# A store behind the last load: one load instead of two, and a wait on VectorE instead of on the load's first part

## Chip, cores, metric

One core of one Trainium2 chip. The metric is the device time of one execution in microseconds (us); the median over several executions is quoted. The profile's span runs from the core's first to its last recorded instruction.

## The reference

The first half of each head's 64 elements is rotated by tables of cosines and sines; the second half is passed on.

```python
# x: (16, 512, 16, 64) float32; cos, sin: (512, 32) float32
x1, x2 = x[..., :32], x[..., 32:]
first  = x1[..., :16] * cos[..., :16] - x1[..., 16:] * sin[..., :16]
second = x1[..., :16] * sin[..., :16] + x1[..., 16:] * cos[..., :16]
out = concatenate([first, second, x2], axis=-1)
```

33.5 MB are read and 33.5 MB are written.

## The kernel before

The data are four tiles of 128 partitions x 16 rows (64 KB a partition, 8 MB a tile). A ring in SBUF has three slots, so tile 3 goes into tile 0's slot once tile 0 is stored. VectorE rotates a tile in place, in two pieces of 8 rows, with four instructions each. All loads and stores are issued by one queue (SP).

```python
    K = 16; NS = 3; KC = K // 2; KL = 14
    # ...
    load(0)
    load(1)
    load(2, 0, KC)
    # ... tables for cosine and sine ...
    def rotate(t, lo, hi):
        # ...
        nc.vector.tensor_mul(out=b_t, in0=x1, in1=s)            # L96
        nc.vector.tensor_mul(out=x1, in0=x1, in1=c)             # L97
        nc.vector.tensor_sub(out=x1[..., 0:Q], ...)             # L98
        nc.vector.tensor_add(out=x1[..., Q:HF], ...)            # L101

    def turn(t):
        rotate(t, 0, KC)
        rotate(t, KC, K)
        return store(t)

    turn(0)
    load(2, KC, K)
    near = load(3, 0, KL)
    load(3, KL, K)
    tc.add_manual_dep(turn(1).ins, near.ins.name, ...,   # the store of tile 1 waits for `near`
        reason="the store follows the loads at the DMA engines")
    turn(2)
    turn(3)
```

The queue's order is load 0, 1, half of 2, store 0, the other half of 2, load 3 (14 rows, then 2), store 1, 2, 3. Nothing in the data makes store 1 wait for load 3; only the declared dependence does.

Of the kernel before, what the change touches and what calls it, by code (L numbers as in the profile page):

```python
# [1 line left out]

# [4 lines left out]


@with_exitstack
def kernel(  # L10
    ctx: ExitStack,
    tc: tile.TileContext,
    x: bass.AP,
    cos: bass.AP,
    sin: bass.AP,
    out: bass.AP,
):
    nc = tc.nc
    fp32 = mybir.dt.float32
    P = 128  # L20
    B, S, H, D = x.shape
    Q = D // 4
    HF = D // 2



    K = 16
    T = B * S // (P * K)
    PB = S // K
    REP = P // PB  # L30
    R = H * D
    NS = 3
    KC = K // 2
    KL = 14

    xf = x.rearrange("b s h d -> (b s h d)").rearrange("(t p f) -> t p f", t=T, p=P)
    of = out.rearrange("b s h d -> (b s h d)").rearrange("(t p f) -> t p f", t=T, p=P)
    cosf = cos.rearrange("(p k) j -> p (k j)", k=K)
    sinf = sin.rearrange("(p k) j -> p (k j)", k=K)

    const_pool = ctx.enter_context(tc.tile_pool(name="const", bufs=1))
    b_pool = ctx.enter_context(tc.tile_pool(name="bp", bufs=1, space=bass.MemoryType.PSUM))


    ring = const_pool.tile([P, NS, K, H, D], fp32)
    stage = const_pool.tile([P, 2, K, HF], fp32)
    spun = const_pool.tile([P, 2 * K, Q], fp32)
    packed = const_pool.tile([PB, 2 * K, Q], fp32)
    table = const_pool.tile([P, 2, K, 2, Q], fp32)

    def rows(t, lo, hi):
        return ring[:, t % NS, lo:hi].rearrange("p k h d -> p (k h d)")

    def load(t, lo=0, hi=K):
        return nc.sync.dma_start(out=rows(t, lo, hi), in_=xf[t, :, lo * R : hi * R])

    def store(t, lo=0, hi=K):
        return nc.sync.dma_start(out=of[t, :, lo * R : hi * R], in_=rows(t, lo, hi))


    nc.vector.memset(stage[:, :, :, 0:Q], 0.0)  # L61
    spread = stage.rearrange("(j b) t k i -> j b t (k i)", b=REP)
    nc.gpsimd.dma_start(out=spread[:, 0, 0], in_=cosf)  # L63
    nc.gpsimd.dma_start(out=spread[:, 0, 1], in_=sinf)  # L64
# [7 lines that stand above are left out]
    PQ = PB // REP  # L72
    nc.vector.stream_shuffle(  # L73
        out=spun[:],
        in_=stage.rearrange("p t k j -> p (t k) j")[:, :, 0:Q],
        mask=[j % PQ * REP for j in range(PB)],
    )
    for q in reversed(range(REP)):
        n = PQ * (q + 1)
        nc.vector.tensor_copy(out=packed[0:n], in_=spun[q * PB : q * PB + n])  # L80

    for r in range(REP):
        nc.vector.tensor_copy(  # L83
            out=table[r * PB : (r + 1) * PB].rearrange("p t k c j -> p (t k) c j"),
            in_=packed.unsqueeze(2).to_broadcast((PB, 2 * K, 2, Q)),
        )
    C = table[:, 0].rearrange("p k c j -> p k (c j)")
    Sn = table[:, 1].rearrange("p k c j -> p k (c j)")

    def rotate(t, lo, hi):  # L90
        x1 = ring[:, t % NS, lo:hi, :, 0:HF]
        c = C[:, lo:hi].unsqueeze(2).to_broadcast((P, hi - lo, H, HF))
        s = Sn[:, lo:hi].unsqueeze(2).to_broadcast((P, hi - lo, H, HF))
        b_full = b_pool.tile([P, KC, H, HF], fp32, name="b_t")
        b_t = b_full[:, 0 : hi - lo]
        nc.vector.tensor_mul(out=b_t, in0=x1, in1=s)  # L96
        nc.vector.tensor_mul(out=x1, in0=x1, in1=c)  # L97
        nc.vector.tensor_sub(  # L98
            out=x1[:, :, :, 0:Q], in0=x1[:, :, :, 0:Q], in1=b_t[:, :, :, Q:HF]
        )  # L100
        nc.vector.tensor_add(  # L101
            out=x1[:, :, :, Q:HF], in0=x1[:, :, :, Q:HF], in1=b_t[:, :, :, 0:Q]
        )

    def turn(t):
        rotate(t, 0, KC)
        rotate(t, KC, K)
        return store(t)

    turn(0)  # L110
    load(2, KC, K)
    near = load(3, 0, KL)
    load(3, KL, K)

    tc.add_manual_dep(
        turn(1).ins,
        near.ins.name,
        mybir.DependencyInfo(mybir.DependencyClass.Sync, mybir.DependencyReason.DATA),
        reason="the store follows the loads at the DMA engines",
    )  # L120
    turn(2)
    turn(3)


# [1 line left out]
_INS = ['x', 'cos', 'sin']  # L126
_OUTS = [((16, 512, 16, 64), 'float32')]


# [23 lines left out]
```

## Time and profile before

| | before |
|---|---|
| time, median (6 runs) | 161.45 us (161.37 to 161.53) |
| span of the profile | 160.3 us, on a run of 162.1 us |
| DMA queue, share of 16 engines | 97.6% |
| VectorE busy | 112.4 us, 70% |

The lines are in the prediction below. VectorE matters only through when it lets the queue issue something. The profile fell on an execution 0.6 us slower than the median.

### The profile page before, as it was taken

The numbers are of one execution on the slowest core, as the hardware profiler recorded it, in microseconds if no ns is written. First come the engines' busy times: TensorE is split into PE (matmuls) and PEld (weight loads), VectorE is DVE, ScalarE is ACT, GpSimd is POOL, SyncE is SP. The second block draws the span as 40 slices with busy tenths as digits, with TensorE's granted clock in tenths as the row PEclk, the third lists the DMA queues.
The fourth block names the chain that finished last, engine by engine and source line by source line (L and its number), as shares of the span: only waits on it lengthen the run. The fifth ranks groups of instructions, "written<-read, shape, count | busy, mean of one in ns | idle before, by whom it ended". The sixth has DMA issues, their size and how long they took to land.

```text
span 160.3 us, 113 instructions
## 1 busy us (share of the span) xinstructions
DVE 112.4 (70%) x43; POOL 1.4 (1%) x6
## 2 busy tenths in 40 slices
DVE  1000959999999999999999999999999950000000
POOL 3000000000000000000000000000000000000000
DMA  7969969699699996999999995996996996996990
GB/s 262 540 262 540 491 294 523 278 507 491 294 392 441 474 523 262 523 392 392 499 482 458 458 444 253 546 523 262 523 523 262 523 507 278 523 507 278 523 507 16
DMA packets 1504, 67.24 MB, mean 419 GB/s; under 512 B 192, under 2 KB 192, under 8 KB 224
## 3 DMA queue, kind: packets, MB, share of 16 engines
q1 hardware_dynamic: 1440, 67.11, 97.6%
q0 software_dynamic: 64, 0.13, 0.2%
HBM read 33.69 MB, written 33.55 MB: 419 GB/s over the span
## 4 chain that ended last, share of the span: by engine, by line
DVE 59%; DMA 14%; issue 7%; DVEq 1%
DVE b_t L96 22%; DVE ring L97 22%; DMA ring<-in_x_dram 14%; DVE ring L101 10%; DVE ring L98 4%; DVEq L148 1%; DVEq L96 0%
## 5 line engine op out<-in xcount | busy, mean ns | idle before, releaser
L96 DVE TENSOR_TENSOR b_t<-ring,table 128x4096 f32<-128x4096 f32 x8 | 35.5, 4432 | 2.1 <-DMA ring<-in_x_dram 1.9
L97 DVE TENSOR_TENSOR ring<-ring,table 128x4096 f32<-128x4096 f32 x8 | 35.4, 4424 | 0.3
L98 DVE TENSOR_TENSOR ring<-ring,b_t 128x2048 f32<-128x2048 f32 x8 | 18.3, 2287 | 0.3
L101 DVE TENSOR_TENSOR ring<-ring,b_t 128x2048 f32<-128x2048 f32 x8 | 18.2, 2280 | 0.0
L73 DVE LOAD_MASK_SELECT spun<-stage x1 | 0.0, 14 | 14.4 <-DMA stage<-in_sin_dram 14.4
L83 DVE COPY table<-packed 32x1024 f32<-32x1024 f32 x4 | 2.7, 684 | 0.1
L80 DVE COPY packed<-spun 32x512 f32<-32x512 f32 (+3 forms) x4 | 1.7, 416 | 0.1
L61 DVE MEMSET stage<- 128x512 f32 x1 | 0.5, 485 | 0.9 <-PEq L137 0.9
L73 DVE STREAM_SHUFFLE spun<-stage 128x512 f32<-128x512 f32 x1 | 0.7, 723 | 0.0
L63 POOL DMA_DIRECT2D stage<-in_cos_dram x1 | 0.6, 649 | 1.3 <-DVE stage L61 1.3
L64 POOL DMA_DIRECT2D stage<-in_sin_dram x1 | 0.5, 532 | 0.0
L137 POOL MEMSET const-float32-0.0<- 128x1 f32 x1 | 0.1, 93 | 0.2 <-issue 0.2
L137 POOL MEMSET const-bfloat16-1.0<- 128x1 bf16 x1 | 0.1, 95 | 0.0
L137 POOL MEMSET const-uint8-127<- 128x1 uint8 x1 | 0.1, 93 | 0.0
L137 POOL MEMSET const-float32-1.0<- 128x1 f32 x1 | 0.1, 92 | 0.0
## 6 DMA issues: line engine op xcount, KB each, us to landing
ring<-in_x_dram SPq DMA_DIRECT2D x2, 4096.0 KB, 41.4
ring<-in_x_dram SPq DMA_DIRECT2D x1, 7168.0 KB, 26.4
ring<-in_x_dram SPq DMA_DIRECT2D x1, 1024.0 KB, 28.5
stage<-in_cos_dram POOLq DMA_DIRECT2D x1, 64.0 KB, 9.0
stage<-in_sin_dram POOLq DMA_DIRECT2D x1, 64.0 KB, 13.4
out_dram<-ring SPq DMA_DIRECT2D x4, 25.6
ring<-in_x_dram SPq DMA_DIRECT2D x2, 32.0
```

What stands on the lines that cost most here:

```text
L61: nc.vector.memset(stage[:, :, :, 0:Q], 0.0)
L63: nc.gpsimd.dma_start(out=spread[:, 0, 0], in_=cosf)
L64: nc.gpsimd.dma_start(out=spread[:, 0, 1], in_=sinf)
L73: nc.vector.stream_shuffle(out=spun[:], in_=stage.rearrange("p t k j -> p (t k) j")[:, :, 0:Q], mask=[j % PQ * REP for j in range(PB)],)
L80: nc.vector.tensor_copy(out=packed[0:n], in_=spun[q * PB : q * PB + n])
L83: nc.vector.tensor_copy(out=table[r * PB : (r + 1) * PB].rearrange("p t k c j -> p (t k) c j"), in_=packed.unsqueeze(2).to_broadcast((PB, ...
L96: nc.vector.tensor_mul(out=b_t, in0=x1, in1=s)
L97: nc.vector.tensor_mul(out=x1, in0=x1, in1=c)
L98: nc.vector.tensor_sub(out=x1[:, :, :, 0:Q], in0=x1[:, :, :, 0:Q], in1=b_t[:, :, :, Q:HF])
L101: nc.vector.tensor_add(out=x1[:, :, :, Q:HF], in0=x1[:, :, :, Q:HF], in1=b_t[:, :, :, 0:Q])
L137: nc = _bacc.Bacc("TRN2", target_bir_lowering=False, num_devices=1)
L148: with _tile.TileContext(nc) as tc:
```

## The change

The last load goes out whole, which saves a DMA of small packets. The store behind it, which must not come late, is released by a point in VectorE's work on tile 2 that falls shortly before the load's end. To have such a point, the second half of tile 2 is rotated in two pieces, rows 8 to 12 and 13 to 15.

```diff
-    KL = 14
+    KM = 13
...
-    turn(0)
+    rotate(0, 0, KC)
+    rotate(0, KC, K)
+    store(0)
     load(2, KC, K)
-    near = load(3, 0, KL)
-    load(3, KL, K)
+    load(3)
+    rotate(1, 0, KC)
+    rotate(1, KC, K)
+    behind_loads = store(1)
+    rotate(2, 0, KC)
+    near = rotate(2, KC, KM)      # rotate now returns its last instruction
+    rotate(2, KM, K)
+    store(2)
     tc.add_manual_dep(
-        turn(1).ins,
+        behind_loads.ins,
         near.ins.name, ...
```

More of the change, by code (lines that the diff above doesn't have):

```diff
@@ L100, in rotate @@
         )
-        nc.vector.tensor_add(
+        return nc.vector.tensor_add(
             out=x1[:, :, :, Q:HF], in0=x1[:, :, :, Q:HF], in1=b_t[:, :, :, 0:Q]
         )
-    def turn(t):
-        rotate(t, 0, KC)
-        rotate(t, KC, K)
-        return store(t)
-    turn(0)
-    load(2, KC, K)
-    near = load(3, 0, KL)
-    load(3, KL, K)
+    rotate(0, 0, KC)
+    rotate(0, KC, K)
+    store(0)
+    load(2, KC, K)
+    load(3)
[6 more added lines that the diff above has]
+    store(2)
     tc.add_manual_dep(
-        turn(1).ins,
+        behind_loads.ins,
         near.ins.name,
@@ L120 @@
     )
-    turn(2)
-    turn(3)
+    rotate(3, 0, KC)
+    rotate(3, KC, K)
+    store(3)
 _INS = ['x', 'cos', 'sin']
```

## The prediction

> **What bounds the kernel now.** I read the page's header, its rows by slice and its queue table first, to see which resource is full.
>
> ```profile
> span 160.3 us, 113 instructions
> ...
> DVE 112.4 (70%) x43; POOL 1.4 (1%) x6
> ...
> DVE  1000959999999999999999999999999950000000
> ...
> GB/s 262 540 262 540 491 294 523 278 507 491 294 392 441 474 523 262 523 392 392 499 482 458 458 444 253 546 523 262 523 523 262 523 507 278 523 507 278 523 507 16
> DMA packets 1504, 67.24 MB, mean 419 GB/s; under 512 B 192, under 2 KB 192, under 8 KB 224
> ...
> q1 hardware_dynamic: 1440, 67.11, 97.6%
> ```
>
> One DMA queue fills 97.6% of sixteen engines over the whole span, while VectorE is busy for 70% and stops a fifth before the end. The jumping GB/s row is only an artefact: whole packets are counted in the slice in which they begin. Averaged over nearly the whole stream the engines are full:
>
> ```profile
> core 0: us, DVE busy (x) POOL busy (x), PEclk, DMA share, GB/s
> 2.30:158.40 156.10, 111.87 (x42) 0.58 (x2) 1.00 0.99 425
> ...
> 158.40:160.30 1.90, 0.00 (x0) 0.00 (x0) 1.00 0.00 0
> ```
>
> In the single packet records of the trace I looked for holes. There are none after the start: a 65,536-byte packet takes 2.418 us and the next on its engine starts 2.414 us after it, whether load or store, from the first packet at 1.74 us to the last store data at 158.4 to 158.9 us. So the span is 1.7 us of start, about 157 us of uninterrupted stream, and about 1.5 us of last landing and closing. The chain of waits on the page names VectorE for 59%, but it is a poor guide here: it ends in VectorE's last instruction and does not follow the last store. The queue's own waits and the order of issues tell more.
>
> ```profile
> SPq L58 <- DMA ring<-in_x_dram: 46.5, 2, 25.6
> SPq L148 <- DMA out_dram<-ring: 28.3, 1, 28.3
> ...
> ring<-in_x_dram SPq DMA_DIRECT2D x1, 7168.0 KB, 26.4
> ring<-in_x_dram SPq DMA_DIRECT2D x1, 1024.0 KB, 28.5
> ```
>
> The 25.6 us wait is the one that the change replaces: the store of tile 1 stands behind the first 14 rows of the last load. The timeline dates it (start, duration):
>
> ```profile
> 72.47 0.80 SPq L55 DMA_DIRECT2D ring<-in_x_dram  x2
> ...
> 90.28 4.43 DVE L96 TENSOR_TENSOR b_t<-ring,table 128x4096 f32<-128x4096 f32 x1
> 94.75 4.42 DVE L97 TENSOR_TENSOR ring<-ring,table 128x4096 f32<-128x4096 f32 x1
> ...
> 98.96 0.34 SPq L58 DMA_DIRECT2D out_dram<-ring  x1
> ...
> 103.72 0.34 SPq L58 DMA_DIRECT2D out_dram<-ring  x1
> ...
> 130.61 0.33 SPq L58 DMA_DIRECT2D out_dram<-ring  x1
> ```
>
> The two loads go out at 72.47 us and, with the queue's earlier load still moving, their data follow in order. The 14-row part lands at 98.89 us (72.47 + 26.4), the store is issued at 98.96, and the 2-row tail, 1 MB, is still moving until 100.45 to 100.90 us, engine by engine. On every engine the store's first packet starts within 0.01 us of the tail's completion packet. The tail exists to cover the time between issue and first packet; it does so completely.
>
> **What the Trainium skill says.** "DMA: Bandwidth & Descriptors", section "Where 436 GB/s comes from", puts the ceiling of sixteen ports at 435.2 GB/s. Sixteen packets of 65,536 bytes every 2.414 us are 434.4 GB/s, so the trace agrees, and the stream has no rate left to gain. The same page, section "Latency and other measured facts", gives about 600 ns to the first byte of such a DMA; here the first load is issued at 0.74 us and its first packets start at 1.74 to 2.40 us on the sixteen engines, so 1.0 to 1.66 us, and I use that. "VectorE: DVE Perf Modes", section "The TRN2 errata — SBUF-src ops pay a fixed extra latency per instruction", has (N + 151) / 0.96 ns for an fp32 tensor-tensor instruction: for 4,096 elements 4,424 ns, which is L97's measured mean; for 2,048 it gives 2,291 ns against 2,287 and 2,280. I use it for the new sizes. "Perfetto Trace Analysis", section "Per-instruction lifecycle: what the profiler-reported window actually captures", says that the profiled window of such a DMA leaves out the data movement; the trace agrees, 0.34 us of issue against 21.8 us to landing for this store.
>
> **The change part by part.**
>
> *The load in one piece.* Removed: one DMA issue on the queue (0.43 us, while the queue has 9 us of the earlier load's data to move, so off the path) and sixteen completion packets. Per engine, eight packets of 57,344 bytes at a spacing of 2.113 us and eight of 8,192 at 0.306 us are 16.90 + 2.45 = 19.35 us; eight of 65,536 at 2.414 us are 19.31. That is 0.04 us less; the completion packet, 0.006 us until the next starts, makes 0.05 us. This is on the path, since the stream has no hole. The load's data should then end at about 100.40 to 100.85 us.
>
> *The new wait.* Rows 8 to 12 of tile 2 are two multiplications over 5 x 512 = 2,560 elements, (2,560 + 151) / 0.96 = 2,824 ns each, and a subtraction and an addition over 1,280, 1,491 ns each: 8.63 us. The old eight rows sum to 4.43 + 4.42 + 2.29 + 2.28 = 13.42 us and take 13.44 from 90.28 to 103.72, so the instructions stand end to end and the sum may be taken as elapsed time. VectorE's point is 90.28 + 8.63 = 98.91 us; with the 0.03 us seen between tile 2's last instruction (101.41 + 2.28 = 103.69) and its store's issue (103.72), the store goes out at 98.94 us. The old one went at 98.96. The new wait therefore releases the store within some hundredths of the old one, with the stream ending some hundredths earlier: the lead is 1.46 us where it was 1.49.
>
> *The extra split.* Rows 13 to 15 need 1,536 elements, 1,757 ns twice, and 768, 957 ns twice: 5.43 us. Tile 2 is done at 98.91 + 5.43 = 104.34 instead of 103.69 us, 0.65 us later, which is four more instructions at 151 / 0.96 = 157 ns each (0.63) and rounding. Tile 3 and its store shift to about 131.2 us. Neither is on the path: the store of tile 1 has eight packets an engine, 19.3 us from 100.4, so the store of tile 2 is needed at about 119.7 less 1.7, and has 13 us to spare; that of tile 3 is needed at about 139.0 less 1.7, and has 6 us. Tile 3's load lands at about 101.3 us, 3 us before VectorE wants it.
>
> *Sum:* -0.05 us from the packets, 0.00 from the wait, 0.00 from the split. Of 161.49 that leaves 161.44 us.
>
> **The rivals.**
>
> *The new point is late.* It is timed to the end of the load by arithmetic, not tied to it, so every tenth by which the store misses the load's end is a tenth on all sixteen engines and on the time. For it: issue to first packet was as much as 1.66 us on some engines at the start, and 98.94 + 1.66 = 100.60 us lies behind 100.40, when the earliest engine falls free. Against it: the old lead was nearly the same and left no hole. If it bites, 0.1 to 0.2 us: 161.6. It would need VectorE's point a whole 3 us later to pass 2%.
>
> *The store also still waits for the whole load.* Then it would be issued at about 101.3 us and start at 102.3 or later, some 1.9 us after the engines fell free: 163.4 us, 1.2% slower. Against it: the store reads another slot of the ring than the load writes, the loads were no obstacle beyond the declared dependence, and only that dependence is moved.
>
> *VectorE becomes the bound.* Its 0.65 us would appear in full only if the last store were waited for. The 6 us of room before the third store say no: 161.44 as it stands.
>
> *The smaller parts were dearer than the packets show*, for instance by a hole between the two loads. The packet records show 0.006 to 0.009 us there, so the gain can't be above a tenth.
>
> **Range and chances.** All terms are below 0.2 us, and the three runs of before differ by 0.11 us. Between runs and chips I allow half a microsecond, and a little more upwards for the late store. I predict 161.44 us, between 161.0 and 162.0 eight times in ten. To be 2% faster the kernel would have to come to 158.2, below the time of the bare stream with its start and end; to be 2% slower it would need a 3.2 us hole. Chances: 0.01 faster, 0.97 within 2%, 0.02 slower.
>
> **What would show it.** The queue's waits should show the 25.6 us wait on the load gone and one on VectorE's L101 in its place. The store of tile 1 should issue at 98.8 to 99.1 us, tile 2's at about 104.3 and tile 3's at about 131.2. The load should be one issue of 8 MB that lands at about 101.3, the hardware queue should count 1,440 - 144 = 1,296 packets, and VectorE's busy time should rise by about 0.6 us to 113. The packets should stand without a hole at 100.4 us. A hole there, or a store issued after 99.5 us, would make the timing step wrong; a span that falls by over 0.3 us would mean that the split load had a cost that the packets don't show.

## The result

| | before | after |
|---|---|---|
| time, median of 6 runs | 161.45 us (161.37 to 161.53) | 161.67 us (161.48 to 161.94) |
| profiled span | 160.3 us (run of 162.1) | 159.6 us (run of 161.73) |

The ratio is 1.0014, 95% interval 1.0001 to 1.0027. A ratio is the mean time of one kernel's runs over that of the other's of the same rounds, so not quite the ratio of the medians. In two further sets of runs it was 1.0002 (0.9989 to 1.0016) and 1.0012 (1.0000 to 1.0025). The change is worth nothing; if anything it costs 0.1 to 0.2 us.

The page after, its header, engine row and queue row:

```profile
span 159.6 us, 114 instructions
...
DVE 112.9 (71%) x47; POOL 1.4 (1%) x6
...
q1 hardware_dynamic: 1296, 67.11, 97.8%
```

The queue's waits after (engine and line, what was waited for, total us, how often, the longest):

```profile
SPq L58 <- DVE ring L101: 85.2, 4, 26.9
...
SPq L58 <- DMA ring<-in_x_dram: 20.9, 1, 20.9
```

The timeline after (start, duration), from the last instruction of the new piece to the end of tile 2, and tile 3's store:

```profile
97.39 1.48 DVE L101 TENSOR_TENSOR ring<-ring,b_t 128x1280 f32<-128x1280 f32 x1
98.90 5.79 SPq L58 DMA_DIRECT2D out_dram<-ring  x2
...
103.37 0.95 DVE L101 TENSOR_TENSOR ring<-ring,b_t 128x768 f32<-128x768 f32 x1
104.35 4.43 DVE L96 TENSOR_TENSOR b_t<-ring,table 128x4096 f32<-128x4096 f32 x1
...
131.24 0.33 SPq L58 DMA_DIRECT2D out_dram<-ring  x1
```

The wait of 25.6 us on the load is gone and VectorE's L101 has taken its place; the wait of 20.9 us that is left is the one for tile 0's load at the start. The point fell at 98.87 us (97.39 + 1.48) and the store was issued at 98.90. The row "x2" merges the stores of tiles 1 and 2, at 98.90 and 104.34. The single packet records of the trace, which no view prints one by one, show the rest. On the first engine (here and below, the one that falls free first) the whole load's data run from 80.52 to 99.84 us. The store's first packet starts 0.02 us later, and no engine stands idle for more than 0.03 us: no hole worth the name.

The span is 0.7 us shorter than in the profile of before, but that is not the change. Most of it arose before the two programs differ: when the data of tile 3's load began, the profile of after was already 0.50 us ahead. The same stretch of time in both traces, before first, then after (in these rows: stretch, its length, VectorE and POOL busy, clock, DMA share of the engines, GB/s; packets count where they begin):

```profile
24.00:41.40 17.40, 17.26 (x6) 0.00 (x0) 1.00 1.02 422
```

```profile
24.00:41.40 17.40, 17.26 (x6) 0.00 (x0) 1.00 0.97 422
```

The same bytes took 0.05 x 17.4 = 0.87 us more of each engine's time before (0.78 us by the packet records, where 96 packets took 2.46 to 2.71 us instead of 2.418). These are packets of tile 1's load, which both kernels issue alike at 1.2 us. The profile of before shows a slow execution. A second one was therefore taken.

### The profile page after: what moved, and what is told of

Same layout as the page of the kernel before. It is cut to its first block, busy times and chain, and to the rows that moved or that the text cites. A ratio compares the mean times of both kernels' runs of the same rounds, so it can differ in the third digit from the quotient of the medians. Undisturbed runs are those within 1.5% of the kernel's fastest.

```text
span 159.6 us, 114 instructions
## 1 busy us (share of the span) xinstructions
DVE 112.9 (71%) x47; POOL 1.4 (1%) x6
## 3 DMA queue, kind: packets, MB, share of 16 engines
q1 hardware_dynamic: 1296, 67.11, 97.8%
## 4 chain that ended last, share of the span: by engine, by line
DVE 61%; DMA 14%; issue 5%; DVEq 1%
DVE b_t L96 22%; DVE ring L97 22%; DMA ring<-in_x_dram 14%; DVE ring L101 10%; DVE ring L98 7%; DVEq L152 1%; DVEq L96 0%
## 5 line engine op out<-in xcount | busy, mean ns | idle before, releaser
L96 DVE TENSOR_TENSOR b_t<-ring,table 128x4096 f32<-128x4096 f32 (+2 forms) x9 | 35.6, 3959 | 2.1 <-DMA ring<-in_x_dram 1.9
L97 DVE TENSOR_TENSOR ring<-ring,table 128x4096 f32<-128x4096 f32 (+2 forms) x9 | 35.6, 3950 | 0.3
L98 DVE TENSOR_TENSOR ring<-ring,b_t 128x2048 f32<-128x2048 f32 (+2 forms) x9 | 18.4, 2050 | 0.3
L101 DVE TENSOR_TENSOR ring<-ring,b_t 128x2048 f32<-128x2048 f32 (+2 forms) x9 | 18.4, 2043 | 0.0
```

The source lines that it names most:

```text
L98: nc.vector.tensor_sub(out=x1[:, :, :, 0:Q], in0=x1[:, :, :, 0:Q], in1=b_t[:, :, :, Q:HF])
L101: return nc.vector.tensor_add(out=x1[:, :, :, Q:HF], in0=x1[:, :, :, Q:HF], in1=b_t[:, :, :, 0:Q])
```

## The experiments

Twelve runs were made in three sets of four; each set shared a chip and nine executions of the kernel before. Their results together ("outside" is the mean of time less span; for before it was 1.77 to 1.79 in every set):

| run | set | time, median | ratio to before (95%) | mean span | outside |
|---|---|---|---|---|---|
| changed kernel | 1 | 161.65 | 1.0002 (0.9989 to 1.0016) | 159.64 | 1.97 |
| point after 12 rows | 1 | 162.02 | 1.0030 (1.0016 to 1.0044) | 160.02 | 2.03 |
| point after 14 rows | 1 | 163.15 | 1.0092 (1.0078 to 1.0106) | 161.03 | 2.04 |
| changed, no dependence | 1 | 162.64 | 1.0067 (1.0054 to 1.0079) | 160.64 | 2.01 |
| before, once more | 2 | 161.46 | 0.9995 (0.9983 to 1.0008) | 159.72 | 1.76 |
| before, with VectorE's split | 2 | 162.02 | 1.0027 (1.0013 to 1.0041) | 159.80 | 2.20 |
| changed, load in two | 2 | 162.00 | 1.0030 (1.0017 to 1.0042) | 159.84 | 2.20 |
| before, store 0 in two too | 2 | 162.25 | 1.0044 (1.0031 to 1.0057) | 160.08 | 2.19 |
| changed kernel | 3 | 161.65 | 1.0012 (1.0000 to 1.0025) | 159.68 | 2.01 |
| changed, no split | 3 | 161.93 | 1.0025 (1.0012 to 1.0039) | 159.74 | 2.17 |
| before, no dependence | 3 | 162.54 | 1.0065 (1.0052 to 1.0078) | 160.78 | 1.75 |
| store behind the whole load | 3 | 166.42 | 1.0305 (1.0290 to 1.0319) | 164.25 | 2.16 |

The mean span of before in the three sets was 159.78, 159.77 and 159.73 us.

My first theory (A) was that the store now comes too late in a typical run, because the profile I had predicted from was slow ahead of it. The rivals were mere scatter (B), a cost of the added VectorE instructions (C), and, for the run without the dependence, that a store already in the queue disturbs the load in front of it (D).

**The changed kernel again.** No edit.

> The changed kernel once more, to see whether its 0.2 us over the kernel before hold on another set of runs. Theory A (late store: the profile of before that I predicted from had slow packets at 24 to 52 us; without them the stream reaches the end of the last load some 0.6 to 0.9 us earlier, at about 99.5 to 99.8 us, while VectorE's point stays at 98.9, so the store's lead falls under the 1 us or so that a first packet needs): 0.15 to 0.3 us over before, and in the trace first store packets 0.0 to 0.3 us behind the end of the load. Theory B (scatter of runs, nothing real): within 0.05 us of before. Theory C (the four added VectorE instructions cost): 0.2 us over before, with no hole in the stream.

161.65 us, 0.05 us over before by the means, so the 0.2 us were not seen here. In the trace the store is issued at 98.79 us, the load's data end at 99.76 on the first engine, and the store's packet follows within 0.01 us. The lead had indeed shrunk to 0.97 us, as A says; but there was no hole, so A's consequence did not follow.

**The point one row earlier.**

```diff
-    KM = 13
+    KM = 12
```

> One row fewer before the point, so by the instruction formula it falls at 97.3 us instead of 98.9 and the store has 1.6 us more lead; four VectorE instructions are added as in the changed kernel. Theory A: the time falls by 0.2 to 0.3 us below the changed kernel's, to 161.35 to 161.45, level with before or 0.05 under it. Theory B: the same as the changed kernel within 0.05 us. Theory C: as the changed kernel, since the split costs as much.

All three missed. The time rose by 0.44 us over the changed kernel (mean times, 162.05 against 161.61), and the span by 0.38. The earlier store harmed. Between 97 and 100 us the last load packets of this kernel start:

```profile
97.00:100.00 3.00, 2.93 (x3) 0.00 (x0) 1.00 0.92 350
```

For the same 350 GB/s the next kernel's row has a share of 0.81. The difference, 0.11 x 3 us = 0.33 us an engine, is lost in the load's last packets: in the records fourteen of the sixteen took 2.55 to 3.15 us, where 2.418 us is the rule (0.34 us an engine in all).

**The point one row later.**

```diff
-    KM = 13
+    KM = 14
```

> One row more before the point, which moves to 100.5 us. Theory A: the whole 1.6 us show as a hole in the DMA stream, since the lead was used up already: 163.2 us or more, 1.5 to 1.7 over the changed kernel. If the prediction's lead were right (1.46 us before the end of the load at 100.4), some 0.4 us of it would be to spare and the loss only about 1.1 us: 162.7. Theory C: as with A or the lead, it says nothing on this one.

The row of the same stretch as above, and the issue in the timeline:

```profile
97.00:100.00 3.00, 2.97 (x3) 0.00 (x0) 1.00 0.81 350
```

```profile
100.51 0.34 SPq L58 DMA_DIRECT2D out_dram<-ring  x1
```

The store was issued at 100.51 us, 1.61 later, and the span grew by 1.39 us, less than A's 1.5 to 1.7 and more than the 1.1 that the prediction's lead would have given. Here the queue was empty, so the trace shows what a store needs from issue to first packet: 0.84 us on the quickest engine, 0.99 on the slowest (101.35 to 101.50). The mean hole over the sixteen engines is 1.28 us. The packets of the three stores behind it were a little slow as well, 0.19 us an engine over the rule of 2.418 us a packet, against 0.03 to 0.05 in the changed kernel.

**The changed kernel without the dependence.**

```diff
-    tc.add_manual_dep(behind_loads.ins, near.ins.name, ...)
```

> The changed kernel with the declared dependence taken away: the store of tile 1 goes out as soon as tile 1 is rotated, at 76.8 us, with the earlier load and the last load still queued before it. Theory A: the queue is in order on every engine, so the early store just waits its turn: 161.35 to 161.45, as with 12 rows. Rival D (the dependence was there because a store queued behind a moving load takes bandwidth from it or starts between its packets): 0.3 us or more slower than with 12 rows, with store packets before the load's end.

D came true in the time: by the means the kernel was 0.60 us slower than with 12 rows and 1.04 slower than the changed kernel, 1.00 of it in the span. Its form was not quite D's: no store packet starts before the load's end on its engine. Instead each engine's last load packet takes 2.93 to 3.84 us. The issue in the timeline, and the row of the same stretch:

```profile
76.80 0.34 SPq L58 DMA_DIRECT2D out_dram<-ring  x1
```

```profile
97.00:100.00 3.00, 2.97 (x3) 0.00 (x0) 1.00 1.13 350
```

At the same 350 GB/s the share is 1.13 against 0.81: 0.32 x 3 us = 0.96 us. So the declared dependence is worth about 1 us (in the kernel before too, as a run further down shows), and the time has a minimum in the store's lead (from issue to the end of the load on the first engine): no loss at 0.94 to 0.97 us, 0.34 us of stretched packets at 2.68, 0.97 us at 23.9, a hole of 1.28 us at -0.54.

**The kernel before again.** No edit.

> The kernel before, unchanged, as a run of its own: the control of the method, and a second profile (the first fell on a run of 162.1 us, 0.6 above the median). Expected: ratio 1.000 within 0.001, span 159.7 to 159.9, 1.7 to 1.85 us between span and time, no instruction packet after the span, and no slow packets at 24 to 52 us; the packets at 68 us, where the second half of tile 2's load follows the store of tile 0, should be slow by 0.3 to 0.5 us an engine as in all the other profiles, if that is not a matter of the change.

As expected in every number: ratio 0.9995, span 159.75 us in its profile. The slow packets at 24 us were gone, and those at 68 us were there (0.5 us an engine), so they are not of the change. The timeline, with the stores of tiles 1 and 2 merged in one row:

```profile
98.42 5.63 SPq L58 DMA_DIRECT2D out_dram<-ring  x2
```

The store was issued at 98.42 us instead of 98.96, and the load's data ended at 99.97 instead of 100.45. The lead was 1.55 us where the first profile had 1.49. A wait on the first part of the load moves with the stream. VectorE's point does not: 98.90 us in the changed kernel, whose load ended at 99.84.

**The split on VectorE alone, in the kernel before.**

```diff
-    turn(2)
+    rotate(2, 0, KC)
+    rotate(2, KC, 13)
+    rotate(2, 13, K)
+    store(2)
```

> The kernel before with the extra split of tile 2 on VectorE alone (8, 5 and 3 rows); load and wait as before. Theory E (the four VectorE instructions more make the program fetch one more block of 8,192 bytes of instructions after its end, as the profiles of all four kernels with the split show and before does not; it lies outside the span): span as before, 159.6 to 160.0, but the time 0.2 us longer, 161.7 to 161.8, with 2.0 us between span and time, and the packet after the span. Theory C (the split costs in the stream): the span grows as well. Theory B: no difference.

The span stayed (159.80 against 159.77 us), so the four instructions cost nothing within it: as a cost in the stream, C is out. The time rose by 0.46 us all the same, more than E's 0.2, of which 0.42 lie outside the span (2.20 us against 1.78). The instruction packet of 8,192 bytes after the span is in the trace. That looked like theory E, but three other runs contradict it.

**The changed kernel with the load in two.**

```diff
-    load(3)
+    load(3, 0, 14)
+    load(3, 14, K)
```

> The changed kernel with the last load again in 14 and 2 rows, the wait on VectorE kept: what the whole load is worth by itself. From the packets: 0.05 us slower in the span than the changed kernel (159.65), so 159.7; and 2.0 us between span and time, 161.7. If the tail of small packets shields the load's end from the queued store, the same; if small packets are worse there, 0.1 to 0.3 more.

Mean span 159.84 us (159.7 to 160.1), 0.07 over before of the same runs, where the changed kernel was 0.14 and 0.05 under before in its own. The whole load is worth 0.1 to 0.2 us in the span by this, with a scatter of the same size; the packet records, 19.32 us of data an engine against 19.36, carry only 0.04 of it. The time missed what was expected, 162.0 against 161.7: 2.20 us lie outside the span, not 2.0.

**The same trick at the other turn.** An attempt to beat both: the stretch at 68 us is where the second half of tile 2's load follows the store of tile 0.

```diff
-    turn(0)
-    load(2, KC, K)
+    rotate(0, 0, KC)
+    rotate(0, KC, K)
+    near_store = store(0, 0, KL)
+    store(0, KL, K)
+    tc.add_manual_dep(load(2, KC, K).ins, near_store.ins.name, ...)
```

> A version that should beat both: the kernel before with the same trick at the other turn of direction. The store of tile 0 goes out in 14 and 2 rows, and the second half of tile 2's load waits for the 14 rows to land instead of being queued at once behind the store. Theory D (a DMA of the other direction that is already queued stretches the last packets of the one in front; 0.3 to 0.45 us an engine at 68 us in all profiles of the changed family, 0.97 at 96 us without the dependence): the slow packets at 68 us vanish, span 159.3 to 159.5, time 161.1 to 161.3, 0.2 to 0.4 under before. Rival: the slow packets there belong to the memory and not to the queue; then the same as before, or slower by a hole if the load comes late. It adds one DMA issue.

It failed. The load was issued at 68.96 us, 1.57 before the store's end, and the store's own packets became regular, but the load's first packets became slow in their place: 0.44 us an engine in all, against 0.52 without the trick. So from store to load a lead of 1.57 us, which cost nothing from load to store, did not remove the loss; what causes it is open. The time rose by 0.7 us, of which 0.4 outside the span. There was no instruction packet after this span, although 2.19 us lie outside it: the first contradiction to E.

**The changed kernel a third time.** No edit.

> The changed kernel a third time, on one chip with the three below, because what lies between span and time was 2.0 us on one chip and 2.2 on another for kernels with the split. Expected: span 159.6 to 159.7, about 0.1 under before's; between span and time 2.0 to 2.2 us against before's 1.77; time 0.1 to 0.3 us over before.

As expected: mean span 159.68 us, 0.05 under before, 2.01 us outside against 1.77, time 0.18 over before by the means. The issue at 98.90 us led the load's end at 99.86 by 0.96 us.

**Without the split: the point on an instruction that is there anyway.**

```diff
-    near = rotate(2, KC, KM)      # returned its addition
-    rotate(2, KM, K)
+    near = rotate(2, KC, K)       # returns its second multiplication
```

> The changed kernel without the extra split: the load whole, and the store waits for an instruction that is there anyway, the second multiplication of tile 2's second half, which ends at 99.2 us instead of 98.9. If the time outside the span comes with the four added instructions (theory E), 1.77 us lie between span and time again. The store's lead over the load's end is about 0.65 us instead of 0.94, so up to 0.3 us of hole in the stream: span 159.6 to 159.9, time 161.4 to 161.7, at best 0.1 under before. If the time outside came from the whole load or the new wait, it stays 2.0 or more, and the time is 161.7 or more.

The span is as expected, 159.74 us: the store was issued at 99.25 us, the first engine was free at 99.88, the store's first packet on any engine came 0.24 us later, and the mean hole is 0.09 us. But 2.17 us lie outside, without the split and without an instruction packet behind the span. E is refuted as it stood: the long time outside appears without the four instructions too. In the kernel before they alone raised it by 0.42 us, so they are one way to it and not the only one; the cause stays open.

**The kernel before without its dependence.**

```diff
-    tc.add_manual_dep(turn(1).ins, near.ins.name, ...)
+    turn(1)
```

> The kernel before with the dependence taken away and the load still in 14 and 2 rows: the store of tile 1 goes out at 76.8 us. No split, so about 1.77 us between span and time. Theory D (a queued store stretches the last packets of the load in front): if the stretch goes by the last packets, the sixteen-engine mean of it should again be about 1 us, now over small packets: span 160.6 to 160.9, 162.3 to 162.7 us. If it goes by the number of bytes or packets in flight and the small packets are a shield: less than 0.5 us.

D came true again: the span is 1.05 us longer than before (160.78 against 159.73), with 1.75 us outside. Small packets are no shield: the stretch, 0.84 us an engine, lies in 67 packets of 8,192 bytes that took up to 0.99 us instead of 0.31. The rows of this kernel and of the control:

```profile
97.00:101.50 4.50, 4.47 (x3) 0.00 (x0) 1.00 1.28 466
```

```profile
97.00:101.50 4.50, 4.46 (x3) 0.00 (x0) 1.00 1.09 466
```

The same bytes, and 0.19 x 4.5 us = 0.86 us more busy time.

**The store behind the whole load.**

```diff
-    load(3)
+    near = load(3)
...
-    near = rotate(2, KC, KM)
-    rotate(2, KM, K)
+    rotate(2, KC, K)
```

> The load whole and the store behind its landing, no split: what the cover is worth, and the prediction's second rival made real. The load lands at about 100.7, 0.9 us after the first engine is free; the first store packet needs about 1 us from the issue. The hole should be 1.3 to 1.9 us on each engine, so span 161.0 to 161.6; with 1.77 us outside the span 162.8 to 163.4 us.

This kernel did not do what I meant. The queue issued two stores together, as its timeline shows:

```profile
71.83 0.33 SPq L55 DMA_DIRECT2D ring<-in_x_dram  x1
103.60 0.82 SPq L58 DMA_DIRECT2D out_dram<-ring  x2
```

By the semaphores in their records, the first waits for tile 2's loads and the second for load 3: the build had put the store of tile 2 ahead of that of tile 1, so nothing was issued before tile 2 was done. The mean hole is 4.2 us. It confirms the latency (0.84 to 0.99 us again, from 103.60 to 104.44 and 104.59) and leaves open what a wait on the whole load alone would cost.

## Why the prediction was right, and where it was not

The time was 161.67 us, 161.44 predicted, and the mechanism held in the main: the store is released about where it was, and nothing else is on the path. That no hole opened was luck, as told below. By its steps:

- **The bound.** Right. The stream stayed full, and every change of mean span over 0.35 us in the experiments was a hole, or in the runs with an early store a stretch, in the DMA packets.
- **The whole load, -0.05 us.** Right as a count: 19.32 us of data an engine against 19.36. In the mean span the changed kernel stands 0.14 and 0.05 us under before, two sets. The sum did not have that the stores behind the load then ran slower: 0.03 to 0.05 us an engine in three profiles of the changed kernel, 0.00 in the second profile of before, which is as much as the load gains. The prediction's sign for a hidden cost of the split load, a span that falls by over 0.3 us, is there between the two first profiles (0.7 us), but falsely: it compares a slow execution with a usual one.
- **VectorE's point.** 98.91 us predicted, 98.87 in the trace, issue 98.90 against 98.94. The later stores came at 104.34 and 131.24 against 104.3 and 131.2, VectorE was busy for 112.9 against 113, and the queue had 1,296 packets. None of the shift reached the end.
- **The lead, "1.46 us where it was 1.49": wrong.** It was 0.94 to 0.97 in three profiles. I took the end of the load from a slow execution and did not ask whether the two ends of that interval move together. That no hole came of it is due to a second wrong term: 1.0 to 1.66 us from issue to first packet, read at the first load of the kernel, where a store later in the kernel needs 0.84 to 0.99 (whether the place or the direction makes the difference was not tested). The two errors cancelled by luck, with nothing to spare: in the changed kernel one engine already stood idle for 0.03 us, and with a lead of 0.62 us the first store packet came 0.24 us after the first engine fell free.
- **Two readings of the packet records: wrong.** Not every packet of 65,536 bytes in the profile of before takes 2.418 us: 115 of the 768 took 2.46 to 3.33 us, 96 of them in tile 1's load. These 96 are most of what made that execution slow, and they could have been seen beforehand. And 2.40 us is when the fifteenth engine started; the sixteenth started at 2.61, so 1.0 to 1.66 us should read 1.0 to 1.87.
- **The rival of the late point.** Its slope was near enough: 1.61 us later made 1.28 us of hole. A store that waits for the whole load was never seen as such.
- **A missing rival.** The prediction treats an early store as free. It never asks why the dependence was declared, though the code says it. The change sits in a valley with two walls, and 1.6 us to the left (0.38 us of span) or to the right (1.39 us) both cost.
- **The sum's sign.** -0.05 us were predicted; the measured change is 0.05 to 0.2 us upwards. The span did fall; the time outside it rose from about 1.78 to about 2.0 us in the two sets that hold both kernels, a term that the sum did not have. What sets it is open. It kept its level for a kernel from run to run: 1.75 to 1.79 for the kernel before, its copy, and the one without its dependence; 1.97 to 2.04 for the changed kernel and its three variants of set 1; 2.16 to 2.20 for the other five. None of the split, the whole load and the instruction packet is needed for a high level.

## What to carry to other kernels

Where the DMA engines are full, a store behind a load has a best moment of issue: here 1 to 1.6 us before the load ends (between 1.6 and 2.7 us nothing was measured). Later leaves a hole, and much earlier (2.7 us and more) stretches the last packets of the load in front, so "as early as possible" cost 1 us here. For a load behind a store no such moment was found. A wait on the landing of the load's first part keeps that moment when the stream shifts; a point in VectorE's work, which did not wait for the stream here, stayed where it was (90.28 and 90.26 us for the start of tile 2's second half) while the stream moved by 0.5 us, so take its margin from several profiles, not from one. And look at time less span before explaining a tenth: part of it may lie where no view reaches.

## What the Trainium skill lacked or had wrong

- "DMA: Bandwidth & Descriptors", section "Latency and other measured facts": about 600 ns to the first byte. Here a store on an empty queue started its packets 0.84 to 0.99 us after its issue began (two kernels), and the first load of the kernel before 1.0 to 1.87 us after. Counted from the end of the 0.34 us issue the store's figure is 0.50 to 0.65 us, which would agree; the page does not say from where the 600 ns count.
- The same page, section "Rules for kernel authors", advises, for overlap with compute, to issue a DMA early and to wait on its semaphore late, and names no cost of it. A store queued 24 us ahead of its turn behind a load cost 1.0 us (both with large and with small last packets), and one 2.7 us ahead 0.34 us. No page that I read prices a change from load to store or back; from store to load 0.52 us an engine were lost with the load queued early and 0.44 with a lead of 1.57 us.
- No page that I read says that the time outside the span differs by kernel: 1.77, 2.0 and 2.2 us here, by kernels that differ in a handful of instructions.
